# A two-layer decoder trunk in split fp32r: q and k among the conv blocks, rotation halves swapped on ScalarE, high products ahead of low ones

## The chip, the cores and the metric

The kernel runs on one core of a Trainium2 chip. The metric is the device time of one execution in microseconds, the median of several runs. Engines are named as in the profile: PE (TensorE matmuls), PEld (its weight loads), DVE (VectorE), ACT (ScalarE), POOL (GpSimd), SP (SyncE, which issues the DMA loads).

## The reference, cut to what matters

```python
# T = 256 tokens, D = 1024, 2 layers; 4 retention heads, q/k 128 wide, v 256 wide
def hybrid_layer(x, positions, ...):
    proj = rmsnorm(x, norm_mix) @ w_in            # cb cc cu | q k v g | ga gb
    y_conv = (cb * causal_conv3(cc * cu)) @ w_conv_out
    q, k = rotary(q) * 128**-0.5, rotary(k)       # [t1 cos - t2 sin, t1 sin + t2 cos]
    o = retention(q, k, v)                        # decayed q k^T times v, by chunks
    y_ret = (silu(g) * headnorm(o) * ret_norm) @ w_ret_out
    x = x + (sigmoid(ga) * y_conv + sigmoid(gb) * y_ret) @ w_o
    return x + relu(rmsnorm(x, norm_mlp) @ w_up)**2 @ w_down
```

After two layers a last rmsnorm follows. All is float32.

## The kernel before

The activations stand transposed, features on the 128 partitions and the 256 tokens along the free dimension. A weight block is 1 MB: all 1024 inputs of 256 outputs, 16 tiles of 128x128. SP loads it into one of two `raw` buffers; `split_block` cuts each half of it into a high part (ACT rounds to fp32r, line 103) and a low part (DVE subtracts, line 104) in one of three `parts` buffers.

`window` handles one block. With `i` the block's number it first runs the small work that was put down for this point with `at(n, fn)` (n windows later, in order of `ph`), then splits block i+2, then issues the products of block i, then the load of block i+3, then the small products put down with `products_at`. Each engine has its instructions in exactly this order; nothing is rescheduled. In `proj` a block is 32 products: for each of 8 input tiles k and 2 output tiles j one of the high part with high and low activations side by side (512 columns) and one of the low part with the high activations (256 columns), which adds to the second half of the same PSUM tile. The result of a block is taken in the next window by `collect`: ACT copies one half out of PSUM, DVE adds the other.

A layer is 4 blocks for v (`proj_tokens`, 24 products of 512 columns), 28 in the order of `IN_ORDER`, 4 each for `yc` (conv output), `yr` (retention output) and `mg` (merged), 16 for up, 16 for down. In the last layer the last four down blocks go through `proj_one`, with products of 256 columns only. So 72 and 68 blocks, 140 in all, go through `proj`.

Around `q` and `k`, `rotate` (line 448) collects a block, POOL multiplies by the cosine (L451), DVE multiplies the two swapped halves by the sine, 64 partitions at a time (L453, L454), and POOL adds (L455). The tables are multiplied by the norm factor first (`rotations`). The norm factor comes from column sums on PE (`norm_total`), then `factors_begin` and `factors_end` on DVE. In layer 0 POOL computes the angles (`reduce_angles`) meanwhile; the small tiles of this stage share six buffers (tag `tmp1`). For the heads, `head_sums` sums the squares `osq` on PE into `var_ps`, `head_roots` begins an inverse root on DVE and `head_out` multiplies by it, which gives `yr`.

Of the kernel before, what the change touches and what calls it, by code (L numbers as in the profile page):

```python
# [18 lines left out]
P = 128  # L19
# [15 lines left out]
def _conv(i):  # L35
# [5 lines left out]
    + _conv(0) + _conv(1)  # L41
    + [("q", Q0), ("q", Q0 + 256), ("k", K0), ("k", K0 + 256)]
# [10 lines left out]
def trunk_kernel(ctx, tc, px, pos, w, cst, mask, out):  # L53
# [22 lines left out]
    idle = tmp.tile([P, 2 * T], BF16, tag="tmp1", bufs=6, name="idle")  # L76
# [90 lines left out]
    def proj(act, n_blocks=1):  # L167
# [6 lines left out]
        def products(blk, b):  # L174
            for k in range(KT):
                a = act[b].at(k)
                for j in range(2):
                    first, end = b == 0 and k == 0, b == n_blocks - 1 and k == KT - 1
                    mm(ps[:, j], blk[:, 0, 2 * k + j, :], a, first, False)
                    mm(ps[:, j, 1], blk[:, 1, 2 * k + j, :], a[:, 0], False, end)  # L180
# [76 lines left out]
    class Norm:  # L257
# [33 lines left out]
        def split_sum(self):  # L291
            self.sums = tuple(tmp.tile([P, T], F32R, tag="tmp1", bufs=6, name=f"{self.name}_{n}") for n in ("sh", "sl"))
            split(self.sum[:, 0, :], *self.sums)
# [35 lines left out]
    xs = tmp.tile([P, T], F32, tag="tmp1", bufs=6, name="xs")  # L329
# [32 lines left out]
    def late_loads():  # L362
        pos_i = tab["pos"] = tmp.tile([P, T], I32, tag="tmp1", bufs=6, name="pos_i")
# [7 lines left out]
    def reduce_angles():  # L371
        ang, turns, red = (tmp.tile([P, T], F32, tag="tmp1", bufs=6, name=nm) for nm in ("ang", "turns", "red"))
# [13 lines left out]
    def sines():  # L386
        half_sin = tab["sh"] = tmp.tile([P, T], F32, tag="tmp1", bufs=6, name="sh")
# [14 lines left out]
    for layer in range(DEPTH):  # L402
# [6 lines left out]
        def factors_begin(norm=norm):  # L409
            rs_m, rs_a = (tmp.tile([P, T], F32, tag="tmp1", bufs=6, name=n) for n in ("rs_m", "rs_a"))  # L410
# [19 lines left out]
        if layer == 0:  # L430
# [6 lines left out]
            products_at(5, norm_total)  # L437
        else:
            products_at(2, norm_total)
        at(10, rotations)  # L440
# [8 lines left out]
        def rotate(p, ps, cosr, sinr):  # L449
            t, d = collect(ps), qk[:, 2 * p:2 * p + 2, :]  # L450
            nc.gpsimd.tensor_tensor(out=d, in0=t, in1=both(cosr), op=ALU.mult)  # L451
            w_ = t2("rot")
            nc.vector.tensor_tensor(out=w_[0:64], in0=t[64:128], in1=both(sinr[64:128, :]), op=ALU.mult)  # L453
            nc.vector.tensor_tensor(out=w_[64:128], in0=t[0:64], in1=both(sinr[0:64, :]), op=ALU.mult)  # L454
# [122 lines left out]
        def head_roots(i, st):  # L577
# [10 lines left out]
            at(1, lambda: nc.vector.reciprocal(rs, rs))  # L588
            at(2, lambda: newton(rs, t2("rs_a", "rs", 1), rm[:, 1, h, :]))
            for n in range(2):  # L590
                at(2 + n, head_out, 2 * i + n, rs[:, n, :])
# [306 lines left out]
```

## Time and profile before

| what | value |
|---|---|
| median of 3 runs | 906.25 us (905.71 to 907.66) |
| the profiled execution, and its span | 909.5 us, 907.7 us |
| PE busy | 885.3 us, 98% |
| PEld busy | 764.6 us, 84% |
| DVE busy | 709.2 us, 78% |
| ACT busy | 512.9 us, 57% |
| POOL busy | 258.0 us, 28% |
| granted TensorE clock | 0.998 |
| HBM traffic | 179 GB/s over the span |

The span runs from the first instruction to the last; the execution's time has some 2 us around it. A busy share is taken over the whole span, with all its stages. A matmul's end is modelled, so times between products are best read from start to start.

### The profile page before, as it was taken

The page shows a single profiled execution, that of the slowest core. Times are in us where ns is not written, and L with a number is a line of the kernel's source. Part 1 is how long each engine was busy: PE and PEld are TensorE (multiplying, and loading weights), DVE is VectorE, ACT ScalarE, POOL GpSimd, SP SyncE. Part 2 cuts the span into 40 slices and gives each one's busy share as a digit, 9 for nine tenths or more (in the row PEclk, how much of TensorE's full clock was granted, in tenths as well). Part 3 has the DMA queues.
Part 4 walks back from the last instruction along what each step waited for, and adds up shares of the span by engine and source line. Part 5 has one row for each costly group of instructions (what it writes and reads, how often), then busy time and mean ns, then how long its engine had stood idle before and what let it go on. Part 6 is the DMA issues. An engine that isn't in the chain of part 4 may idle for free.

```text
span 907.7 us, 12561 instructions
## 1 busy us (share of the span) xinstructions
PE 885.3 (98%) x5026; PEld 764.6 (84%) x5026; DVE 709.2 (78%) x796; ACT 512.9 (57%) x733; POOL 258.0 (28%) x168
## 2 busy tenths in 40 slices
PE   9988999999999999999999999999999999999996
PEld 6867788878888888888888888888888888888896
DVE  5779999999898766555567999999999896664551
ACT  5835455765556777544445543656665577763350
POOL 0646545422112322100010655452211222220110
PEclk9999999999999999999999999999999999999999
DMA  8534454445654555555555444544465455555531
GB/s 285 189 133 170 168 179 164 183 144 182 232 192 180 195 186 186 197 185 187 187 184 193 156 174 152 190 182 142 159 247 181 185 202 186 186 192 185 183 138 46
DMA packets 23818, 163.00 MB, mean 180 GB/s; under 512 B 2768, under 2 KB 3152, under 8 KB 4432
## 3 DMA queue, kind: packets, MB, share of 16 engines
q1 hardware_dynamic: 23184, 161.36, 50.3%
q10 hardware_dynamic: 576, 0.84, 0.3%
q8 instruction: 39, 0.64, 0.3%
q14 instruction: 19, 0.16, 0.0%
HBM read 161.14 MB, written 1.05 MB: 179 GB/s over the span
## 4 chain that ended last, share of the span: by engine, by line
PE 64%; DVE 23%; issue 4%; POOL 3%; DMA 3%; ACT 2%; SPq 0%; DVEq 0%; ACTq 0%; POOLq 0%
PE ps L165 64%; DVE parts L104 14%; DMA raw<-w 3%; DVE sum L236 2%; DVE rot L454 1%; ACT parts L103 1%; DVE acc L518 1%; DVE yc L104 1%; POOL ta L504 0%; POOL red L369 0%; DVE sg L565 0%; DVE sg L498 0%; DVE acc L521 0%; POOL ang L384 0%; DVE sg L236 0%
## 5 line engine op out<-in xcount | busy, mean ns | idle before, releaser
L104 DVE TENSOR_TENSOR parts<-raw,parts 128x1024 fp32r<-128x1024 f32 x305 | 434.4, 1462 | 90.9 <-ACT parts L103 90.2
L103 ACT CAST parts<-raw 128x1024 fp32r<-128x1024 f32 x305 | 305.9, 1050 | 138.1 <-PE ps L165 85.0
L165 PE MATMUL ps<-mix,parts 128*128 128x512 f32 (+1 forms) x1792 | 322.9, 340 | 11.0 <-DVE parts L104 7.5
L165 PEld LDWEIGHTS ps<-mix,parts 128*128 128x128 f32 x1792 | 274.5, 188 | 54.8 <-DVE parts L104 10.0
L165 PE MATMUL ps<-up,parts 128*128 128x512 f32 (+1 forms) x1088 | 182.3, 330 | 0.0
L165 PE MATMUL ps<-mlp,parts 128*128 128x512 f32 (+1 forms) x1024 | 181.6, 340 | 0.0
L165 PEld LDWEIGHTS ps<-up,parts 128*128 128x128 f32 x1088 | 160.6, 189 | 21.1
L165 PEld LDWEIGHTS ps<-mlp,parts 128*128 128x128 f32 x1024 | 157.0, 188 | 23.8
L236 DVE TENSOR_TENSOR sum<-ps,sum 128x512 f32<-128x512 f32 x78 | 53.3, 684 | 45.5 <-ACT sum L235 45.3
L730 POOL TENSOR_TENSOR u<-u,rr2m 128x512 f32<-128x512 f32 x32 | 46.1, 1441 | 131.3 <-ACT u L729 118.3
L235 ACT COPY sum<-ps 128x512 f32<-128x512 f32 x78 | 45.3, 581 | 51.3 <-PE ps L165 51.3
L285 POOL TENSOR_TENSOR mix_sum<-mix_sum,sq 128x512 f32<-128x512 f32 x8 | 12.6, 1574 | 155.7 <-ACT sq L283 155.6
L165 PE MATMUL ps<-yc,parts 128*128 128x512 f32 (+1 forms) x256 | 45.6, 340 | 0.0
L165 PE MATMUL ps<-yr,parts 128*128 128x512 f32 (+1 forms) x256 | 45.5, 340 | 0.0
L165 PE MATMUL ps<-mg,parts 128*128 128x512 f32 (+1 forms) x256 | 45.5, 340 | 0.0
L165 PEld LDWEIGHTS ps<-yr,parts 128*128 128x128 f32 x256 | 39.2, 188 | 6.0
L165 PEld LDWEIGHTS ps<-yc,parts 128*128 128x128 f32 x256 | 39.2, 188 | 6.0
L165 PEld LDWEIGHTS ps<-mg,parts 128*128 128x128 f32 x256 | 39.2, 188 | 6.0
L165 PE MATMUL ps<-parts,mix 128*128 128x512 f32 x180 | 41.8, 392 | 0.0
L165 PEld LDWEIGHTS ps<-parts,mix 128*128 128x128 f32 x180 | 33.6, 188 | 7.4 <-ACT mix L271 0.2
L694 DVE SCALAR_TENSOR_TENSOR px_sb<-ps,px_sb 128x256 f32<-128x256 f32 x60 | 24.0, 421 | 15.6 <-PE ps L165 14.6
L642 POOL TENSOR_TENSOR sum<-sum,rr 128x512 f32<-128x512 f32 x8 | 15.8, 1979 | 59.2 <-DVE sum L236 59.2
(175 smaller groups left out, 668.1 us busy)
## 6 DMA issues: line engine op xcount, KB each, us to landing
raw<-w SPq DMA_DIRECT2D x151, 1024.0 KB, 4.8
raw<-w SPq DMA_DIRECT2D x2, 256.0 KB, 4.4
raw<-w SPq DMA_DIRECT2D x1, 512.0 KB, 5.6
px_sb<-px SPq DMA_DIRECT2D x1, 512.0 KB, 8.3
mask_sb<-mask SPq DMA_DIRECT2D x1, 512.0 KB, 5.7
out<-o SPq DMA_DIRECT2D x2, 256.0 KB, 2.4
out<-o ACTq DMA_DIRECT2D x2, 256.0 KB, 2.4
px_sb<-px SPq DMA_DIRECT2D x1, 256.0 KB, 5.8
```

Source lines behind the costliest of these rows:

```text
L103: nc.scalar.copy(hi, src)
L104: nc.vector.tensor_tensor(out=lo, in0=src, in1=hi.bitcast(F32), op=ALU.subtract)
L165: nc.tensor.matmul(o, lhsT=a, rhs=b, start=start, stop=stop, skip_group_check=True)
L235: nc.scalar.copy(t, ps[:, :, 1, :])
L236: nc.vector.tensor_tensor(out=t, in0=ps[:, :, 0, :], in1=t, op=ALU.add)
L285: nc.gpsimd.tensor_tensor(out=self.sum, in0=self.sum, in1=sq, op=ALU.add)
L454: nc.vector.tensor_tensor(out=w_[64:128], in0=t[0:64], in1=both(sinr[0:64, :]), op=ALU.mult)
L518: nc.vector.scalar_tensor_tensor(out=acc[:, j, 1:], in0=z[:, j, :T - 1], scalar=w1, in1=acc[:, j, 1:], op0=ALU.mult, op1=ALU.add)
L642: nc.gpsimd.tensor_tensor(out=z, in0=z, in1=both(rr2), op=ALU.mult)
L694: nc.vector.scalar_tensor_tensor(out=xk, in0=ps[:, j, half, :], scalar=scale, in1=xk, op0=ALU.mult, op1=ALU.add)
L730: nc.gpsimd.tensor_tensor(out=u, in0=u, in1=both(rr2), op=ALU.mult)
```

## The change

Six edits. In `proj` the products of a block are issued all high parts first (16 of 512 columns), then all low parts (16 of 256); the first block of `yr`, `mg` and up in each layer (`late`) keeps the order before. q, q, k move from behind the second group of conv blocks to between its blocks. `rotate` now only collects and multiplies by the cosine; one window later `rotate_halves` has ACT copy the two halves across, and POOL multiply by the sine and add; the sign of the table is turned round for this. `head_out` multiplies on POOL, and the reciprocal and what follows it come a window later, the reciprocal between the two halves of a split. The column sums of the norm come after the sixth block of a layer in both layers (in the second it was the third), the tables one window earlier. Scores come one window later. `tmp1` has seven buffers.

```diff
 IN_ORDER = (
     [("g", G0), ("g", G0 + 256)]
-    + _conv(0) + _conv(1)
-    + [("q", Q0), ("q", Q0 + 256), ("k", K0), ("k", K0 + 256)]
+    + _conv(0)
+    + [e for qk, c in zip((("q", Q0), ("q", Q0 + 256), ("k", K0)), _conv(1)) for e in (qk, c)]
+    + [("k", K0 + 256)]
     + _conv(2) + _conv(3)
...
-    def proj(act, n_blocks=1):
+    def proj(act, n_blocks=1, late=False):
...
         def products(blk, b):
-            for k in range(KT):
+            kj = [(k, j) for k in range(KT) for j in range(2)]
+            both_parts = [(k, j, part) for k, j in kj for part in range(2)]
+            for k, j, part in both_parts if late else sorted(both_parts, key=lambda e: e[2]):
                 a = act[b].at(k)
-                for j in range(2):
-                    first, end = b == 0 and k == 0, b == n_blocks - 1 and k == KT - 1
+                first, end = b == 0 and k == 0, b == n_blocks - 1 and k == KT - 1
+                if part == 0:
                     mm(ps[:, j], blk[:, 0, 2 * k + j, :], a, first, False)
+                else:
                     mm(ps[:, j, 1], blk[:, 1, 2 * k + j, :], a[:, 0], False, end)
...
-            products_at(5, norm_total)
-        else:
-            products_at(2, norm_total)
-        at(10, rotations)
+        products_at(5, norm_total)
+        at(9, rotations)
...
             nc.gpsimd.tensor_tensor(out=d, in0=t, in1=both(cosr), op=ALU.mult)
-            w_ = t2("rot")
-            nc.vector.tensor_tensor(out=w_[0:64], in0=t[64:128], in1=both(sinr[64:128, :]), op=ALU.mult)
-            nc.vector.tensor_tensor(out=w_[64:128], in0=t[0:64], in1=both(sinr[0:64, :]), op=ALU.mult)
+            at(1, rotate_halves, p, t, sinr)
+
+        def rotate_halves(p, t, sinr):
+            w_, d = t2("rot"), qk[:, 2 * p:2 * p + 2, :]
+            nc.scalar.copy(w_[0:64], t[64:128])
+            nc.scalar.copy(w_[64:128], t[0:64])
+            nc.gpsimd.tensor_tensor(out=w_, in0=w_, in1=both(sinr), op=ALU.mult)
             nc.gpsimd.tensor_tensor(out=d, in0=d, in1=w_, op=ALU.add)
...
-            at(1, lambda: nc.vector.reciprocal(rs, rs))
-            at(2, lambda: newton(rs, t2("rs_a", "rs", 1), rm[:, 1, h, :]))
+            at(2, lambda: nc.vector.reciprocal(rs, rs), ph=1)
+            at(3, lambda: newton(rs, t2("rs_a", "rs", 1), rm[:, 1, h, :]))
             for n in range(2):
-                at(2 + n, head_out, 2 * i + n, rs[:, n, :])
+                at(3 + n, head_out, 2 * i + n, rs[:, n, :])
...
-            nc.vector.tensor_tensor(out=y, in0=y, in1=both(rs), op=ALU.mult)
+            nc.gpsimd.tensor_tensor(out=y, in0=y, in1=both(rs), op=ALU.mult)
...
-                    products_at(1 + h, scores, h)
+                    products_at(2 + h, scores, h)
...
-            at(0, merge_ret if p < NPAIR - 1 else merge_last, p, proj([yr]))
+            at(0, merge_ret if p < NPAIR - 1 else merge_last, p, proj([yr], late=p == 0))
...
-            at(0, add_to_x, p, proj([mg]), 0.5, norm)
+            at(0, add_to_x, p, proj([mg], late=p == 0), 0.5, norm)
...
-            at(0, up_out, p, proj([norm.act]))
+            at(0, up_out, p, proj([norm.act], late=p == 0))
...
-    cst[:half, 1], cst[half:, 1] = 2.0, -2.0
+    cst[:half, 1], cst[half:, 1] = -2.0, 2.0
```

The first place is PE in a block of `proj`; these are the first products of the g block before, its input tiles 0 to 3 in `mix_103`, the other four in `mix_104`.

```order
L165 MATMUL ps<-mix_103,parts 128x512
L165 MATMUL ps<-mix_103,parts 128x256
L165 MATMUL ps<-mix_103,parts 128x512
L165 MATMUL ps<-mix_103,parts 128x256
L165 MATMUL ps<-mix_103,parts 128x512
L165 MATMUL ps<-mix_103,parts 128x256
```

And this is that whole block and the next one in the change.

```order
L166 MATMUL ps<-mix_103,parts 128x512 x8
L166 MATMUL ps<-mix_104,parts 128x512 x8
L166 MATMUL ps<-mix_103,parts 128x256 x8
L166 MATMUL ps<-mix_104,parts 128x256 x8
L166 MATMUL ps<-mix_103,parts 128x512 x8
L166 MATMUL ps<-mix_104,parts 128x512 x8
L166 MATMUL ps<-mix_103,parts 128x256 x8
L166 MATMUL ps<-mix_104,parts 128x256 x8
```

The two sizes, which took turns, now stand in runs of sixteen. The second place is DVE at the first q blocks of layer 0 (`sum` is a collected block, `rot` the swapped halves, `parts` the low halves of a weight block); before:

```order
L236 TENSOR_TENSOR sum<-ps,sum 128x512
L453 TENSOR_TENSOR rot<-sum,sinq 64x512
L454 TENSOR_TENSOR rot<-sum,sinq 64x512
L104 TENSOR_TENSOR parts<-raw,parts 128x1024 x2
L104 TENSOR_TENSOR q_parts<-qk,q_parts 128x512
L236 TENSOR_TENSOR sum<-ps,sum 128x512
L453 TENSOR_TENSOR rot<-sum,sinq 64x512
L454 TENSOR_TENSOR rot<-sum,sinq 64x512
L104 TENSOR_TENSOR parts<-raw,parts 128x1024 x2
```

In the change, with POOL's rows of the same place behind them:

```order
L242 TENSOR_TENSOR sum<-ps,sum 128x512
L105 TENSOR_TENSOR parts<-raw,parts 128x1024 x2
L242 TENSOR_TENSOR sum<-ps,sum 128x512
L105 TENSOR_TENSOR parts<-raw,parts 128x1024 x2
L105 TENSOR_TENSOR q_parts<-qk,q_parts 128x512
L242 TENSOR_TENSOR sum<-ps,sum 128x512
L105 TENSOR_TENSOR parts<-raw,parts 128x1024 x2
```

```order
L455 TENSOR_TENSOR qk<-sum,cosq 128x512
L462 TENSOR_TENSOR rot<-rot,sinq 128x512
L463 TENSOR_TENSOR qk<-qk,rot 128x512
L650 TENSOR_TENSOR sum<-sum,rr_138 128x512
L455 TENSOR_TENSOR qk<-sum,cosq 128x512
L462 TENSOR_TENSOR rot<-rot,sinq 128x512
L463 TENSOR_TENSOR qk<-qk,rot 128x512
```

The two multiplications have left DVE, POOL has three instructions for a q block where it had two, and a conv block lies between. The third place is DVE around the second sum of squares; before, from the reciprocal of heads 0 and 1 on:

```order
L588 RECIPROCAL rm<-rm 128x512
L565 SCALAR_TENSOR_TENSOR sg<-o_ps,hg,sg 128x256 x2
L236 TENSOR_TENSOR ta<-ps,ta 128x512
L104 TENSOR_TENSOR parts<-raw,parts 128x1024 x2
L241 TENSOR_TENSOR rs_a<-rm 128x512
L242 SCALAR_TENSOR_TENSOR rs_a<-rs_a,rm 128x512
L243 SCALAR_TENSOR_TENSOR rm<-rs_a,rm 128x512
L598 TENSOR_TENSOR sg<-sg,rm 128x512
L104 TENSOR_TENSOR osq<-osq 128x256
```

In the change:

```order
L573 SCALAR_TENSOR_TENSOR sg<-o_ps,hg,sg 128x256 x2
L242 TENSOR_TENSOR ta<-ps,ta 128x512
L105 TENSOR_TENSOR parts<-raw,parts 128x1024 x2
L105 TENSOR_TENSOR osq<-osq 128x256
L242 TENSOR_TENSOR ta<-ps,ta 128x512
L105 TENSOR_TENSOR parts<-raw,parts 128x1024
L596 RECIPROCAL rm<-rm 128x512
L105 TENSOR_TENSOR parts<-raw,parts 128x1024
L247 TENSOR_TENSOR rs_a<-rm 128x512
```

The last split of squares stood behind the reciprocal and the four instructions of its root; now it stands ahead of them.

## Rows read from the trace of the kernel before

**Rows 1.** The page: the span, and each engine's busy time.

```profile
span 907.7 us, 12561 instructions
PE 885.3 (98%) x5026; PEld 764.6 (84%) x5026; DVE 709.2 (78%) x796; ACT 512.9 (57%) x733; POOL 258.0 (28%) x168
```

**Rows 2.** PE in order of time: start, length, instructions, idle before; three stretches.

```profile
209.52 22.78 PE L165 MATMUL ps<-yc,parts 128*128 128x512 f32 x128
232.14 22.77 PE L165 MATMUL ps<-yr,parts 128*128 128x512 f32 x128
...
458.50 16.51 PE L165 MATMUL ps<-parts,mix 128*128 128x512 f32 x72
474.84 0.28 PE L165 MATMUL mix_st<-mix_sh,ones 128*128 128x256 f32 x1
...
880.05 5.92 PE L165 MATMUL ps<-up,parts 128*128 128x256 f32 x48
885.81 0.50 PE L758 MATMUL st<-ones_f,mix_sum 128*128 128x1 f32 x4
```

**Rows 3.** PE in order of time in the first projections of layer 0.

```profile
40.53 11.26 PE L165 MATMUL ps<-mix,parts 128*128 128x512 f32 x64
...
53.60 5.60 PE L165 MATMUL ps<-mix,parts 128*128 128x256 f32 x31 [0.58 <-DVE parts L104]
...
120.54 0.52 PE L165 MATMUL sc_ps<-q_parts,k_parts 128*128 128x256 f32 x3
...
121.04 0.48 PE L165 MATMUL ps<-mix,parts 128*128 128x512 f32 x1
...
127.88 5.80 PE L165 MATMUL ps<-mix,parts 128*128 128x512 f32 x32
```

**Rows 4.** Busy time by stretch: PE, PEld, DVE, ACT, POOL; then clock, DMA share, GB/s.

```profile
60.00:106.00 46.00, 40.50 (x222) 34.01 (x223) 43.23 (x41) 24.23 (x33) 31.16 (x19) 1.00 0.45 161
...
525.00:548.00 23.00, 23.00 (x132) 19.97 (x131) 22.77 (x21) 10.08 (x15) 13.02 (x7) 1.00 0.48 177
720.00:870.00 150.00, 150.00 (x851) 130.20 (x850) 93.63 (x98) 90.23 (x122) 29.12 (x21) 1.00 0.54 188
```

**Rows 5.** DVE and POOL in order of time over one q block of layer 0.

```profile
102.97 0.68 DVE L104 TENSOR_TENSOR q_parts<-qk,q_parts 128x512 fp32r<-128x512 f32 x1
...
104.29 0.69 DVE L453 TENSOR_TENSOR rot<-sum,sinq 64x512 f32<-64x512 f32 x1
104.33 1.80 POOL L451 TENSOR_TENSOR qk<-sum,cosq 128x512 f32<-128x512 f32 x1 [2.36 <-DVE sum L236]
104.99 1.69 DVE L454 TENSOR_TENSOR rot<-sum,sinq 64x512 f32<-64x512 f32 x1
106.71 3.45 DVE L104 TENSOR_TENSOR parts<-raw,parts 128x1024 fp32r<-128x1024 f32 x2
106.83 2.25 POOL L455 TENSOR_TENSOR qk<-qk,rot 128x512 f32<-128x512 f32 x1 [0.69 <-DVE rot L454]
...
110.08 0.68 DVE L104 TENSOR_TENSOR q_parts<-qk,q_parts 128x512 fp32r<-128x512 f32 x1
```

**Rows 6.** DVE in order of time where POOL stands idle.

```profile
662.37 2.36 DVE L104 TENSOR_TENSOR parts<-raw,parts 128x1024 fp32r<-128x1024 f32 x2
```

**Rows 7.** DVE's longest wait between 44 and 60 us: total, times, longest.

```profile
DVE rs_a L241 <- POOL ang L384: 4.2, 1, 4.2
```

**Rows 8.** The heads' factor on DVE: least, median and greatest duration of one (ns).

```profile
L598 DVE TENSOR_TENSOR sg<-sg,rm x8: 678/685/693, 191.2 to 655.3; 128x512 f32<-128x512 f32 x8
```

**Rows 9.** Who waited for whom, whole run: total, times, longest.

```profile
PE ps L165 <- DVE parts L104: 7.5, 8, 1.7
...
PE var_ps L165 <- DVE osq L104: 2.4, 2, 1.6
```

**Rows 10.** The page's groups: busy, mean ns of one, idle before and its cause.

```profile
L235 ACT COPY sum<-ps 128x512 f32<-128x512 f32 x78 | 45.3, 581 | 51.3 <-PE ps L165 51.3
L165 PEld LDWEIGHTS ps<-up,parts 128*128 128x128 f32 x1088 | 160.6, 189 | 21.1
```

More of the change, by code (lines that the diff above doesn't have):

```diff
@@ L75, in trunk_kernel @@
     ones_f = const.tile([P, 1], F32, name="ones_f")
-    idle = tmp.tile([P, 2 * T], BF16, tag="tmp1", bufs=6, name="idle")
+    idle = tmp.tile([P, 2 * T], BF16, tag="tmp1", bufs=7, name="idle")
     cst_sb = const.tile([P, 2], F32, name="cst_sb")
@@ L291, in split_sum @@
         def split_sum(self):
-            self.sums = tuple(tmp.tile([P, T], F32R, tag="tmp1", bufs=6, name=f"{self.name}_{n}") for n in ("sh", "sl"))
+            self.sums = tuple(tmp.tile([P, T], F32R, tag="tmp1", bufs=7, name=f"{self.name}_{n}") for n in ("sh", "sl"))
             split(self.sum[:, 0, :], *self.sums)
@@ L327, in trunk_kernel @@
     nc.scalar.activation(eps2, eps, AF.Square)
-    xs = tmp.tile([P, T], F32, tag="tmp1", bufs=6, name="xs")
+    xs = tmp.tile([P, T], F32, tag="tmp1", bufs=7, name="xs")
     nc.vector.tensor_scalar(out=xs, in0=x[:, 0, :], scalar1=norm.gain[:, 0:1], scalar2=None, op0=ALU.mult)
@@ L362, in late_loads @@
     def late_loads():
-        pos_i = tab["pos"] = tmp.tile([P, T], I32, tag="tmp1", bufs=6, name="pos_i")
+        pos_i = tab["pos"] = tmp.tile([P, T], I32, tag="tmp1", bufs=7, name="pos_i")
         nc.sync.dma_start(out=cst_sb, in_=cst)
@@ L371, in reduce_angles @@
     def reduce_angles():
-        ang, turns, red = (tmp.tile([P, T], F32, tag="tmp1", bufs=6, name=nm) for nm in ("ang", "turns", "red"))
+        ang, turns, red = (tmp.tile([P, T], F32, tag="tmp1", bufs=7, name=nm) for nm in ("ang", "turns", "red"))
         tab.update(ang=ang, turns=turns)
@@ L386, in sines @@
     def sines():
-        half_sin = tab["sh"] = tmp.tile([P, T], F32, tag="tmp1", bufs=6, name="sh")
+        half_sin = tab["sh"] = tmp.tile([P, T], F32, tag="tmp1", bufs=7, name="sh")
         ang, turns = tab["ang"], tab["turns"]
@@ L409, in factors_begin @@
         def factors_begin(norm=norm):
-            rs_m, rs_a = (tmp.tile([P, T], F32, tag="tmp1", bufs=6, name=n) for n in ("rs_m", "rs_a"))
+            rs_m, rs_a = (tmp.tile([P, T], F32, tag="tmp1", bufs=7, name=n) for n in ("rs_m", "rs_a"))
             rsqrt_begin(rr, rs_m, norm.total_ps, 1.0 / D)
@@ L786, in square_last @@
         def square_last(k, ps):
-            sq = tmp.tile([P, T], F32, tag="tmp1", bufs=6, name="sq1")
+            sq = tmp.tile([P, T], F32, tag="tmp1", bufs=7, name="sq1")
             nc.scalar.activation(sq, ps, AF.Square)
```

## The prediction

> **What bounds the kernel now.** I read the busy times first: PE is busy 98% of the span, DVE 78%, ACT 57%, POOL 28% [rows 1]. So a gain must either shorten what PE does or fill the 2% in which it stands. Both are to be found by stage, so I read the stretches next. In the up and down stage (720 to 870 us) PE is busy all the time, while DVE has 94 of 150 us, ACT 90, and the loads half of the DMA time [rows 4]: there the products alone set the pace. PE's own order of time shows that pace: four `yc` blocks, 128 products, take 232.14 - 209.52 = 22.62 us from start to start, which is 5.655 us for a block and 353 ns for a pair of 512 and 256 columns [rows 2].
>
> In the first projections of layer 0 it is otherwise. Between 60 and 106 us DVE is busy 43.2 of 46 us and PE only 40.5 [rows 4]. From 40.53 us (block 6, the first cc) to 127.88 us (block 19) there are 13 blocks and two groups of score products of 121.04 - 120.54 = 0.5 us [rows 3]. At the free pace that is 13 x 5.655 + 1.0 = 74.5 us, and it takes 87.35: PE loses 12.8 us here. Part of it is seen as waits for low parts (7.5 us in 8 waits [rows 9], one of them before 53.60 us [rows 3]), the rest as late starts of blocks, whose PSUM tile is not yet collected. In layer 1, in the same work, PE does not stand although DVE is busy 22.77 of 23 us [rows 4]: there DVE starts the stretch well ahead. Later only the head sums wait, 2.4 us in two waits [rows 9].
>
> **The order of products.** 134 of the 140 blocks through `proj` change (three a layer keep the old order). No row shows a block in the new order, but two show its halves. The v products of layer 1 are 72 products of 512 columns in a row: 474.84 - 458.50 = 16.34 us, 226.9 ns each. In the last two output tiles 48 products of 256 columns stand in a row, each with a weight load of its own: 885.81 - 880.05 = 5.76 us, 120.0 ns each [rows 2]. A new block is then 16 x 226.9 + 16 x 120.0 = 5.55 us against 5.655, and 134 x 0.105 = **14.0 us** less. Below, the bound is nothing, if a product's time depends on what it is and not on its neighbour; I take the rows, since both runs are long and even. What follows PE must keep up: DVE, ACT and the loads have room in the up and down stage [rows 4].
>
> On this the Trainium skill says something else. Its page TensorE: Matmul & The Clock Gate, section Back-to-back issue gap, gives a lone product's gap by its own column count alone; by that the sum of a pair, and so the block, is the same in any order, and this term would be nothing. By the page's formula a pair would take an estimated 325 ns, where the trace has 353, so I hold to the trace.
>
> The new order also moves the need for low parts: the first comes 16 x 0.227 = 3.6 us into the block, the second half's 0.96 us later, at 4.6 us, where it was 16 x 0.177 = 2.8 us. So DVE may be 1.8 us (second half) to 3.6 us (first half) later without stopping PE. It helps once in a stretch where DVE is late throughout. ACT's second high half is needed at 1.8 instead of 2.8 us; ACT is busy 24 of 46 us there [rows 4].
>
> **The buffers.** At 44.9 us DVE waits 4.2 us for POOL to finish the angles, because `rs_a` takes over a `tmp1` buffer that POOL still uses [rows 7]. With seven buffers it takes over that of `pos_i`, which POOL reads only in the first instruction of that chain. All of DVE's work behind it, and with it PE's late blocks, comes 4.2 us earlier. Next late is POOL itself, whose tables are then wanted earlier, but the chain of angles ends before DVE asks for them.
>
> **The rotation.** In a q block before, DVE goes round in 110.08 - 102.97 = 7.11 us: split of the rotated block, add of the collected one, two multiplications (0.69 and 1.69 us), the low halves (3.45 us) [rows 5]. PE's block is 5.655 us, so four rounds cost PE 4 x 1.46 = 5.8 us. The multiplications, 2.38 us, leave. But POOL's work is not free for DVE: the second multiplication, the same as the first, takes 1.00 us more while POOL multiplies beside it, and the pair of low halves 3.45 us beside POOL's add [rows 5] against 2.36 us where POOL is idle [rows 6], 1.09 us more. Two POOL instructions fall on low halves now that did not (the cosine, which lay beside `rot`, and the new product), so DVE takes back 0 to 2.18 us a block. Net relief is 0.2 to 2.38 us a block, 0.8 to 5.8 us for PE in layer 0 (no more than it lost). A conv block now lies between two q or k blocks, and conv blocks with little DVE work fill the round; I take the middle, 3.5 us.
>
> Here the Trainium skill speaks against the change. SBUF — State Buffer, section Who interferes with whom, says that a VectorE instruction with two SBUF inputs contends with a GpSimd instruction that reads SBUF, and that ScalarE waits for no one; by it each new POOL product stops the low splits whenever they meet, the lower end of my 0.2 to 2.38. The trace agrees as to the contention (3.45 against 2.36 us); how often they meet is what no row shows.
>
> ACT gains two copies for a rotation, 16 in all. No row has one of 64 partitions; the copy of 128 takes 0.58 us [rows 10], so 0 to 9.3 us on an engine with 43% idle. A copy stands ahead of the next collect and split in ACT's queue, so these come up to 1.2 us later, and DVE waits for them; that is inside the 3.6 us.
>
> So of the 12.8 us in layer 0: 4.2 from the buffer, 3.5 from the rotation, 1.8 from the later need, **9.5 us**; bounds 4.2 + 0.8 = 5.0 and all 12.8. In layer 1 nothing can be given back, since PE does not stand there.
>
> **The heads.** `head_out` leaves DVE, 8 x 0.685 = 5.5 us [rows 8], and POOL gets eight products of up to 2.25 us, which take back up to 8 x 1.09 = 8.7 us of DVE. PE waits for neither: yr is needed only after the gb and yc blocks. Behind POOL's products stand the gb multiplications, behind them ACT's tanh, its collect and its splits, which PE needs two blocks later. I take nothing; the bound is 2.4 us a layer (the net 1.6 us of DVE, and 0.8 us by which PE is faster over eight blocks). The last split of squares now stands ahead of the root's instructions, and the reciprocal behind it, so the squares come over 2 us earlier (three of some 0.7 us and the factor's 0.685): the **2.4 us** of waits for head sums go, at worst none of it.
>
> **The rest.** Norm sums in layer 1 three blocks later: the factor is first used eight blocks after the layer's start and is ready a block earlier; without that cover a wait of one DVE round. Scores and tables move by a window each, at no price while PE has their inputs. The loads keep their order on SP; 1 MB each 5.55 us instead of 5.655 asks for 2% more than 188 GB/s at half the DMA time [rows 4].
>
> **The sum.** 14.0 + 9.5 + 2.4 = 25.9 us. The profiled execution took 909.5 us, so 883.6 under the profiler; its own time was 3.25 us over the median of 906.25, and against the median the forecast is **880.4 us**.
>
> **The rivals.** (1) The order of products does nothing: a pair costs 353 ns in any order. Then 906.25 - 11.9 = 894.4. (This is the case of the Trainium skill's page on TensorE, above.) For it: no row has the new order; against it: 226.9 + 120.0 = 346.9. (2) POOL takes back what DVE was given: it hits the low halves with each instruction, ACT waits in its queue, and the stretches of gb blocks begin to stand. Then 906.25 - 14.0 - 5.0 - 2.4 + 4.8 = 889.7. For it: the 1.09 us of rows 5 and 6; against it: POOL idles 72% [rows 1]. (3) Slower: low products in a row are shorter than their weight loads. A load takes 189 ns [rows 10]; if each low product took as long, a block is 3.63 + 16 x 0.189 = 6.65 us, one us more, 134 blocks 133 us, and the time 906.25 - 11.9 + 133 = 1027. It decides from 120 + 25.9 / (134 x 16) us, that is 132 ns a product. Against it: 120.0 ns in the last tiles, with a load for each. (4) The change has no effect I can name: 2%.
>
> **How the numbers follow.** Chances: forecast 0.66, rival 1 0.12, rival 2 0.17, rival 3 0.03, no effect 0.02. The forecast alone runs from 906.25 - 14.0 - 2.4 - 12.8 = 877 to 885. The range goes down to 874, since runs of one kernel lie 2 us apart and low products that go to and fro between two PSUM banks may be a little quicker than those of the tail; upwards it takes in rival 2 and most of the way to rival 1: 874 to 893. By the cases: faster by over 0.2% (1.8 us, about what a measurement tells here) 0.95, same 0.02, slower 0.03.
>
> **What the profile after would show.** Right: `yc` and down blocks at 5.55 us from start to start; 13 blocks from the first cc on in some 76 us; no wait of `rs_a` on POOL; no wait of `var_ps`; low halves near 3.45 us still where POOL works. Wrong: blocks at 5.65 (rival 1), waits of PE for low parts or for PSUM in layer 1, or about the first yc blocks (rival 2), low products over 130 ns (rival 3).

## The result, and the profile after

The changed kernel takes 892.8 us (median of four runs, 891.85 to 893.35) where the kernel before took 906.0 in the same session: a ratio of 0.9849 (0.9832 to 0.9866), 13.3 us less. The forecast was 880.4 us in a range of 874 to 893. Sign and range held; half the gain is missing.

First the page: span and busy times, against [rows 1].

```profile
span 890.0 us, 12567 instructions
...
PE 875.0 (98%) x5026; PEld 768.8 (86%) x5026; DVE 705.9 (79%) x772; ACT 523.9 (59%) x749; POOL 294.2 (33%) x184
```

DVE has 24 instructions fewer and only 3.3 us less of work; POOL has 36 us more. PE's busy time fell by 10.3 us, so more than half of the 17.7 us of span is PE's pace, the rest waits.

PE in order of time, against [rows 2, 3]: start, length, instructions, idle before.

```profile
40.71 28.31 PE L166 MATMUL ps<-mix,parts 128*128 128x512 f32 x160
...
73.09 46.37 PE L166 MATMUL ps<-mix,parts 128*128 128x512 f32 x256 [4.07 <-DVE sum L242]
...
199.71 22.43 PE L166 MATMUL ps<-yc,parts 128*128 128x512 f32 x128
221.98 22.55 PE L166 MATMUL ps<-yr,parts 128*128 128x512 f32 x128
244.37 4.63 PE L166 MATMUL ps<-mg,parts 128*128 128x512 f32 x24
250.18 12.09 PE L166 MATMUL ps<-mg,parts 128*128 128x512 f32 x66 [1.18 <-DVE mg L689]
```

Four yc blocks take 221.98 - 199.71 = 22.27 us, 5.567 a block where it was 5.655. From block 6 (first cc) PE needs 79.1 us to block 19, which starts at 119.80, where it was 87.35. One of the two groups of score products that the 87.35 us hold (some 0.5 us each) now falls behind block 19, so for the same work the gain is some 7.7 us and not 8.3. The many short waits for low parts are one long wait for a PSUM tile. Then there is a new wait in the first mg block of layer 0, 1.18 us, with which that block takes 7.33 us instead of 5.65.

All waits of PE after, those of the start and the end of the run left out (total, times, longest): the row on `var_ps` of [rows 9] is gone, and so is that of `rs_a` [rows 7].

```profile
PE ps L166 <- DVE sum L242: 4.1, 1, 4.1
...
PE ps L166 <- DVE mg L689: 1.2, 1, 1.2
```

By place, PE in the profiled executions (909.5 and 891.85 us) is ahead of the kernel before by -0.2 us at block 6, 8.1 at block 19, 9.8 at the first yc block, 9.0 at the first up block, 10.2 at the first down block, 11.9 at layer 1's first g block, 14.9 at its yc blocks, 18.0 at the last tiles. So there are three kinds of gain: 8.3 us in the first projections (7.7 for the same work), some 3.3 us at the head sums of both layers (blocks 28 and 29 fell from 13.63 to 11.58 us, 104 and 105 from 12.82 to 11.58), and a slow drip everywhere else. At the mg blocks 1.7 us are lost.

### The profile page after: what moved, and what is told of

Its sections match the earlier page's. It is cut to its first block, busy times and chain, and to the rows that moved or that the text cites. A ratio compares the mean times of both kernels' runs of the same rounds, so it can differ in the third digit from the quotient of the medians.

```text
span 890.0 us, 12567 instructions
## 1 busy us (share of the span) xinstructions
PE 875.0 (98%) x5026; PEld 768.8 (86%) x5026; DVE 705.9 (79%) x772; ACT 523.9 (59%) x749; POOL 294.2 (33%) x184
## 4 chain that ended last, share of the span: by engine, by line
PE 71%; DVE 17%; POOL 4%; DMA 3%; ACT 2%; issue 2%; SPq 0%; DVEq 0%; ACTq 0%; POOLq 0%
PE ps L166 70%; DVE parts L105 10%; DMA raw<-w 3%; ACT parts L104 1%; DVE sum L242 1%; DVE rm L596 1%; PE o_ps L166 1%; POOL rot L462 1%; POOL qk L455 1%; POOL ta L512 0%; POOL qk L463 0%; DVE acc L526 0%; DVE acc L529 0%; DVE rs_a L247 0%; DVE rs_a L248 0%
## 5 line engine op out<-in xcount | busy, mean ns | idle before, releaser
L166 PE MATMUL ps<-mix,parts 128*128 128x256 f32 (+1 forms) x1792 | 319.0, 339 | 4.9 <-DVE sum L242 4.1
L166 PEld LDWEIGHTS ps<-mix,parts 128*128 128x128 f32 x1792 | 278.6, 190 | 42.9 <-issue 4.2
L166 PE MATMUL ps<-up,parts 128*128 128x256 f32 (+1 forms) x1088 | 179.9, 327 | 0.0
L166 PE MATMUL ps<-mlp,parts 128*128 128x256 f32 (+1 forms) x1024 | 179.0, 337 | 0.0
```

The lines of the kernel that those rows point to most:

```text
L166: nc.tensor.matmul(o, lhsT=a, rhs=b, start=start, stop=stop, skip_group_check=True)
```

## The experiments

In the table, "6 to 19" is the time from the first product of block 6 to that of block 19 of layer 0 in the profile, and the ratio is that to the kernel before in the same session. The first two kernels have two groups of score products in that stretch, the others one.

| kernel | median us (runs) | ratio | 6 to 19 | PE's wait for head sums |
|---|---|---|---|---|
| before_again | 907.98 (902.6 to 910.2) | 1.0002 (0.9977 to 1.0027) | 87.3 | 2.5 |
| group_only | 905.32 (904.0 to 905.8) | 0.9972 (0.9955 to 0.9989) | 85.2 | 6.5 |
| changed kernel | 892.79 (891.9 to 893.4) | 0.9849 (0.9832 to 0.9866) | 79.1 | 0 |
| after_ungrouped | 895.83 (894.2 to 896.6) | 0.9872 (0.9842 to 0.9901) | 80.8 | 0 |
| after_alternating | 890.96 (890.1 to 892.5) | 0.9838 (0.9812 to 0.9864) | 80.7 | 0 |
| after_buf6 | 895.19 (894.5 to 898.8) | 0.9889 (0.9864 to 0.9915) | 82.6 | 0 |
| after_rotate_dve | 897.27 (897.0 to 898.6) | 0.9889 (0.9868 to 0.9910) | 81.8 | 0 |
| after_heads_back | 896.37 (894.6 to 896.7) | 0.9891 (0.9866 to 0.9917) | 79.1 | 4.4 |
| after_heads_mid | 893.61 (893.1 to 894.6) | 0.9850 (0.9826 to 0.9874) | 80.0 | 1.0 |
| after_rot10 | 893.05 (891.9 to 894.1) | 0.9841 (0.9814 to 0.9869) | 78.9 | 0 |
| after_cc_first | 892.73 (891.9 to 893.4) | 0.9854 (0.9829 to 0.9880) | 78.5 | 0 |
| after_tables_pool | 892.80 (891.6 to 893.5) | 0.9836 (0.9815 to 0.9857) | 79.0 | 0 |
| after_gate_mg | 896.52 (895.7 to 896.9) | 0.9879 (0.9851 to 0.9906) | 75.6 | 2.1 |

The changed kernel was timed in the first session only. The differences in us below are of medians from different sessions and chips, between which the median of the kernel before moved from 906.0 to 907.6 us. By the ratios they are 2.1 us and not 3.0 for after_ungrouped, 3.6 and not 2.4 for after_buf6, 3.6 and not 4.5 for after_rotate_dve, 3.8 for after_heads_back and 2.7 and not 3.7 for after_gate_mg. All runs of these five kernels lie above those of the changed kernel, but by the ratios only the interval of after_rotate_dve stands clear of its interval, and those of after_buf6 and after_heads_back just touch it. Where a loss lies is read from one profile of each kernel.

### The order of products: four kernels

**before_again** is the kernel before, unchanged.

> The kernel before, unchanged, for its own scatter. Theory A (the gain of 13.3 us is real in both kernels' medians, and the 909.5 us of the first profiled execution were a chance of that run): about 906 us, and where the profile's blocks of products are slower than 5.655 us or its stalls longer, they tell what a slow execution adds. Theory B (the profiled execution adds some 3 us to each kernel): a profile of 909 us again beside a median of 906.

Its runs lie 8 us apart, and its profile (908.9 us) shows two paces for the same 448 products of the up blocks. PE in order of time, layer 0 and layer 1:

```profile
289.59 79.31 PE L165 MATMUL ps<-mlp,parts 128*128 128x512 f32 x448
368.74 90.61 PE L165 MATMUL ps<-up,parts 128*128 128x512 f32 x512
...
729.27 77.82 PE L165 MATMUL ps<-mlp,parts 128*128 128x512 f32 x448
806.93 72.47 PE L165 MATMUL ps<-up,parts 128*128 128x512 f32 x432
```

From start to start it is 368.74 - 289.59 = 79.15 us for 14 blocks in layer 0, 5.653 a block, and 806.93 - 729.27 = 77.66 us in layer 1, 5.547 a block, nothing between. The granted clock is 1.0 in both. A pair of products costs 353.3 ns at the one pace and 346.7 at the other, and a stretch keeps its pace until a wait or other products come. In the first profile, on which the prediction rests, 103 of the blocks that have no wait and no extra products went at the slow pace and one at the quick pace; here it is 60 and 43. Theory B falls: five of the eleven other runs took longer than the profiled one, so what varies is the kernel, not the profiler. Of theory A the chance is shown, not that slower blocks made the long run, since this profile has fewer of them and is as long: the quick pace brings less than 43 x 0.106 us, as it made PE wait 2.6 us more at layer 1's mg block.

**group_only** is the kernel before with the products in groups and nothing else of the change.

```diff
-            for k in range(KT):
-                for j in range(2):
+            for k, j, part in both_parts if late else sorted(both_parts, key=lambda e: e[2]):
```

> The kernel before with nothing but the order of the products changed. Theory A (grouped blocks take 5.567 us, as in the trace after, against 5.653): 134 x 0.086 = 11.5 us from the pace, and 1 to 3 us more in the first projections, where the low parts are needed later: 891.5 to 893.5 us, which would be all that the whole change gave. Theory B (the order does nothing, the gain came from the other parts): 906 us, blocks of 5.65 us. Theory C (the pace gains 11.5 us but PE, now faster, waits more for DVE elsewhere): 895 to 900 us.

2.2 us less by the medians, though its profile has every grouped block at 5.567 us. Theory C is nearest, and more so than it said. The waits of PE (total, times, longest):

```profile
PE var_ps L165 <- DVE osq L104: 6.5, 2, 4.0
PE ps L165 <- DVE sum L241: 4.6, 2, 2.7
```

PE goes ahead where it may be late with low parts, and stands at the next place where it may not, the head sums: 6.5 us for 2.4 in [rows 9]. The clock takes back more. Behind the second of the waits for `sum` (1.9 us) and behind both of those for the head sums (4.0 and 2.5 us) the granted clock fell to 0.50, the 1.2 GHz level; in the first profile of the kernel before it stayed at full up to the end of the run. Busy time by stretch: PE, PEld, DVE, ACT, POOL; then clock, DMA share, GB/s.

```profile
83.50:86.50 3.00, 3.00 (x9) 2.32 (x8) 3.00 (x3) 1.97 (x2) 1.17 (x2) 0.50 0.00 0
193.20:195.90 2.70, 2.70 (x8) 2.13 (x7) 2.70 (x2) 0.49 (x1) 2.17 (x1) 0.50 0.10 36
629.60:632.80 3.20, 3.20 (x9) 2.42 (x9) 3.20 (x4) 1.57 (x2) 1.58 (x1) 0.50 0.00 0
```

Block 29, behind the first head sum's wait, took 6.93 us and block 105 7.17, where 5.57 is the pace.

**after_ungrouped** was to be the changed kernel in the old order. Its edit (`late=True` as the default) reaches 92 blocks; the 42 yr, mg and up blocks that pass `late` themselves stayed in groups, so the number of blocks in the expectation is wrong.

> The changed kernel with the order of products as before. Theory A (grouping is worth 11.5 us by the pace): 892.8 + 11.5 = 904.3 us, plus up to 3 us of waits for low parts that come back: 904 to 907. The other parts together then gave 0 to 2 us. Theory B (the other parts carry the gain): 893 to 897 us.

It took 3.0 us more by the medians, which the ratios don't tell from nothing. Its projections ran mostly at 5.55 us, its down blocks, which follow grouped blocks, at 5.65.

**after_alternating** has high and low products in turn in all blocks of the changed kernel.

```diff
-    def proj(act, n_blocks=1, late=False):
+    def proj(act, n_blocks=1, late=True):
...
-..., proj([yr], late=p == 0))
+..., proj([yr], late=True))
```

(and the same for mg and up.)

> The changed kernel with high and low products in turn in every block. Theory A (this order has two paces at full clock, 5.547 and 5.653 us a block, and goes from one to the other at a stall, as the profiles of before_again and after_ungrouped show; products in groups have only one, 5.567): runs lie anywhere from 892.8 - 134 x 0.020 = 890 to 892.8 + 134 x 0.086 = 904 us, several us from each other, where runs of the changed kernel lie 1.5 us apart; the profile has whole stretches of blocks at one of the two paces and none between. Theory B (the pace is that of the order alone, 5.653 us): 904 us in every run, with a scatter as small as the changed kernel's.

It is no slower than the changed kernel: 890.96 us, and four of its five runs lie below the lowest of that kernel, though in another session. PE in order of time over the up blocks of layer 0, here and then in the changed kernel:

```profile
280.45 77.81 PE L166 MATMUL ps<-mlp,parts 128*128 128x512 f32 x448
358.11 88.91 PE L166 MATMUL ps<-up,parts 128*128 128x512 f32 x512
```

```profile
279.88 78.09 PE L166 MATMUL ps<-mlp,parts 128*128 128x512 f32 x448
357.81 89.23 PE L166 MATMUL ps<-up,parts 128*128 128x512 f32 x512
```

77.66 us at the quick pace against 77.93 in groups. Here 96 blocks went at the quick pace and 10 at the slow one. The two paces are shown; that its runs would scatter by several us is not so, they lie 2.4 us apart. So in the changed kernel the order of products is worth nothing: groups hold the pace of 5.567 us, and the old order, with most waits gone, falls into its quick pace of 5.547 and loses 1.6 us in the first projections, where it needs low parts early.

### The other parts, undone one at a time

**after_buf6**: six `tmp1` buffers instead of seven.

> The changed kernel with six buffers instead of seven for the tables' intermediates. Theory A (the prediction's: DVE waits 4.2 us again for POOL's angles, all its work in the first projections is later by that): 892.8 + 4.2 = 897. Theory B (half of it, since part of DVE's wait is made up before a block of PE is late): 894.5 to 895.5. Theory C (nothing, another wait stands in its place): 892.8.

The wait is back to the tenth of a us (DVE's waits between 40 and 60 us):

```profile
DVE rs_a L247 <- POOL ang L390: 4.2, 1, 4.2
```

Blocks 6 to 19 take 3.5 us more, and 0.6 us of that return at the mg block of layer 0, which is less late. Of the 3.5 us, 0.6 are block 11, where the granted clock stayed at 0.50 for longer. The median is up by 2.4 us: theory B by the median, between A and B by the profile and the ratio.

**after_rotate_dve**: the rotation's multiplications back on DVE.

```diff
-            at(1, rotate_halves, p, t, sinr)
-...
-            nc.scalar.copy(w_[0:64], t[64:128])
-            nc.scalar.copy(w_[64:128], t[0:64])
-            nc.gpsimd.tensor_tensor(out=w_, in0=w_, in1=both(sinr), op=ALU.mult)
+            nc.vector.tensor_tensor(out=w_[0:64], in0=t[64:128], in1=both(sinr[64:128, :]), op=ALU.mult)
+            nc.vector.tensor_tensor(out=w_[64:128], in0=t[0:64], in1=both(sinr[0:64, :]), op=ALU.mult)
```

> The changed kernel with the rotation of q and k as before: two DVE multiplications instead of two ACT copies and a POOL product, and no window between. Theory A (the prediction's: the rotation off DVE is worth some 3.5 us in layer 0, in bounds of 0.8 to 5.8): 892.8 + 3.5 = 896.3. Theory B (POOL, saturated from 79 to 98 us in the trace after, gives back to DVE as waiting on the low halves what the two multiplications took): 892 to 893.5.

Theory A: 4.5 us more, 2.7 of them between blocks 6 and 19. Some 2.6 us are lost in layer 1, where the kernel before had no wait and the prediction expected no gain: 0.7 us in blocks 92 to 103, and 1.9 us at the mg block, where PE now waits for the last merge as it does in layer 0. PE's waits:

```profile
PE ps L166 <- DVE mg L685: 2.4, 2, 1.2
PE ps L166 <- DVE parts L105: 1.6, 3, 1.0
```

**after_heads_back**: reciprocal, Newton step and scaling of the heads as before.

```diff
-            at(2, lambda: nc.vector.reciprocal(rs, rs), ph=1)
-            at(3, lambda: newton(rs, t2("rs_a", "rs", 1), rm[:, 1, h, :]))
+            at(1, lambda: nc.vector.reciprocal(rs, rs))
+            at(2, lambda: newton(rs, t2("rs_a", "rs", 1), rm[:, 1, h, :]))
...
-            nc.gpsimd.tensor_tensor(out=y, in0=y, in1=both(rs), op=ALU.mult)
+            nc.vector.tensor_tensor(out=y, in0=y, in1=both(rs), op=ALU.mult)
```

> The changed kernel with the head roots and the scaling of the heads as before (reciprocal a block earlier and ahead of the last split of squares, scaling on DVE). Theory A (with the products in groups PE comes to the head sums further ahead of DVE, as in group_only, where these waits took 6.5 instead of 2.4 us): blocks 28 and 104 take 8 to 10 us instead of 6.03, so 4 to 8 us are lost: 897 to 901. Theory B (the heads part is worth what the prediction said, 2.4 us): 895.2. Theory C (its scaling on POOL costs what its order gives, as the late mg block of layer 0 says): within 1 us of 892.8.

3.6 us more, just under A's span; PE's waits for the head sums:

```profile
PE var_ps L166 <- DVE osq L105: 4.4, 2, 3.1
```

The mg block of layer 0 is on time again here (5.65 us), so in the profiles the part gives 6.3 us at the sums of both layers and takes back 1.7. More than 1 us of the 6.3 is the clock: behind the 3.1 us wait it fell to 0.50 here too, and block 29 took 6.72 us.

**after_heads_mid** keeps the reciprocal behind the last split, but a window earlier than the change has it, and scales on DVE.

```diff
-            at(2, lambda: nc.vector.reciprocal(rs, rs), ph=1)
+            at(1, lambda: nc.vector.reciprocal(rs, rs), ph=1)
```

> The changed kernel with the reciprocal still behind the last split of squares, but a window earlier than in the change, and the heads' scaling on DVE. Theory A (the gain of the heads part, 3.6 us by after_heads_back, comes from the order alone, and the late mg block of layer 0, 1.7 us, from the window's delay and POOL): blocks 28 and 104 stay at 6.03 and block 40 at 5.65: 891. Theory B (the delay is what takes the wait away): blocks 28 and 104 at 7 to 10 us, 895 to 897.

Neither: 0.8 us more, which the ratios don't tell from nothing. Its profile is 1.4 us longer, and 0.9 us of that stand at block 11, which the edit doesn't reach (the clock stayed at 0.50 for longer there). The mg block of layer 0 improves from 7.33 to 6.11 us, block 28 goes from 6.03 to 7.34. So of the wait for the head sums (4.4 us) the order takes 3.4 away, and the later window and the scaling on POOL, which were not tried apart, the last 1.0; in layer 0 they lose as much at the merge.

### The wait of 4.1 us in the first projections

I first read it so: the two table products for q stand on DVE, a window earlier than before, between DVE and the sum that collects the PSUM tile of block 8. Three kernels test that.

**after_rot10**

```diff
-        at(9, rotations)
+        at(10, rotations)
```

> The changed kernel with the two table products put back by a window. Theory A (in window 9 they stand between DVE and the sum that collects the PSUM tile of block 8, so that PE waits 4.1 us at block 11 and then has half the clock for 3.4 us, 1.7 us): in window 10 that wait goes or shrinks and the clock stays at full; DVE's 3 us of work remain, so 1.5 to 5 us are gained: 888 to 891. Theory B (DVE is short of time over the whole stretch, and the wait only moves to the next block): 892.8 within 0.8 us, with a wait of about 4 us at block 12.

**after_cc_first**

```diff
-    + [e for qk, c in zip(..., _conv(1)) for e in (qk, c)]
+    + [e for qk, c in zip(..., _conv(1)) for e in (c, qk)]
...
+        at(10, rotations)
```

> The changed kernel with each cc, cu, cb block ahead of its q or k block instead of behind it, and the two table products a window later, so that they are needed a window later too. Theory A (DVE's backlog at blocks 9 to 11 comes from the tables standing in the densest window of layer 0; one window later they meet a block with less work): the waits of blocks 9 to 12 fall from some 6 us to 2 to 3, 888 to 891. Theory B (DVE has the same sum of work up to block 18 and PE waits for it somewhere): 892 to 893.5.

**after_tables_pool**

```diff
-            nc.vector.tensor_tensor(out=cosq, in0=cos_t, in1=rr, op=ALU.mult)
-            nc.vector.tensor_tensor(out=sinq, in0=sin_t, in1=rr, op=ALU.mult)
+            nc.gpsimd.tensor_tensor(out=cosq, in0=cos_t, in1=rr, op=ALU.mult)
+            nc.gpsimd.tensor_tensor(out=sinq, in0=sin_t, in1=rr, op=ALU.mult)
```

(cosk and sink a window later.)

> The changed kernel with the table products of q on POOL too, and those of k a window later. Theory A (the 4.1 us wait at block 11 is the tables' 3.0 us on DVE, ahead of the sum that collects block 8, and the half clock behind it 1.7 us more): DVE gets there 3 us earlier, the wait falls to about 1 us and the clock stays: 888 to 890. Theory B (DVE short of time over the whole stretch, POOL's products slow it as much as its own did): 892 to 893.5, and the wait only moves to block 11 or 12.

All three are within 0.3 us of the changed kernel: theory A fell each time. In after_rot10 the wait became two, of 2.70 and 1.91 us; there and in after_cc_first blocks 6 to 19 gain 0.2 and 0.6 us, and the mg block of layer 0 is 0.7 us later. The third kernel shows what stands behind the tables. POOL, ACT, DVE and PE in order of time around the wait:

```profile
64.44 1.26 POOL L375 TENSOR_SCALAR cos_t<-cos_t 128x256 f32<-128x256 f32 x1
65.67 1.29 POOL L503 TENSOR_TENSOR sg<-sg,rr 128x512 f32<-128x512 f32 x1
...
66.99 0.64 ACT L508 ACTIVATE th<-sg 128x512 f32<-128x512 f32 x1 [4.14 <-POOL sg L503]
...
69.06 0.56 ACT L241 COPY sum<-ps 128x512 f32<-128x512 f32 x1
...
67.66 1.09 DVE L509 SCALAR_TENSOR_TENSOR sg<-th,sg 128x512 f32<-128x512 f32 x1 [2.22 <-ACT th L508]
...
72.35 0.69 DVE L242 TENSOR_TENSOR sum<-ps,sum 128x512 f32<-128x512 f32 x1
...
73.18 40.81 PE L166 MATMUL ps<-mix,parts 128*128 128x512 f32 x224 [3.50 <-DVE sum L242]
```

With the tables gone DVE stands 2.22 us instead, for ACT's tanh; ACT has stood 4.14 us for POOL's gate product, which is queued behind the rotation tables, and the copy with which the collect of block 8 begins (69.06) is queued behind that tanh. Here the wait that PE's row puts down to DVE starts on POOL and passes through two queues. In the changed kernel itself that chain ends a little too early to be seen. ACT and DVE there:

```profile
66.31 0.63 ACT L505 ACTIVATE th<-sg 128x512 f32<-128x512 f32 x1 [4.12 <-POOL sg L500]
...
65.05 1.51 DVE L431 TENSOR_TENSOR cosq<-cos_t,rr 128x256 f32<-128x256 f32 x1 [0.30 <-POOL cos_t L375]
66.48 1.51 DVE L432 TENSOR_TENSOR sinq<-sin_t,rr 128x256 f32<-128x256 f32 x1
67.92 1.23 DVE L506 SCALAR_TENSOR_TENSOR sg<-th,sg 128x512 f32<-128x512 f32 x1
...
70.05 1.37 DVE L529 SCALAR_TENSOR_TENSOR acc<-sum,px_sb,acc 128x254 f32<-128x254 f32 x1
...
72.26 0.69 DVE L242 TENSOR_TENSOR sum<-ps,sum 128x512 f32<-128x512 f32 x1
```

The tanh ends at 66.94 and the second table product at 67.99, and from 65.05 to the collect at 72.26 DVE doesn't stand. So two chains end within about 1 us of each other, DVE's own queue last; with the tables gone the other one shows.

**after_gate_mg** moves the first two gates out of the way, and has a second edit: half of a split goes behind the last merge.

```diff
-                at(0, gate, n, ps, 3 if n < 2 else 0)
+                at(0, gate, n, ps, 14 if n < 2 else 0)
...
+        if i - 1 in hold:
+            split_half(i + 1, 1)
...
-        if i > 2:
+        if i > 2 and i not in hold:
```

(`hold` has the window of each layer's last yr block.)

> The changed kernel with the first two gates' POOL product, tanh and DVE product 11 blocks later, and the second half split of the second mg block behind the last merge instead of ahead of it. Theory A (after after_tables_pool: what holds block 8's PSUM tile is ACT's queue, whose tanh waits 4.1 us for POOL's gate product behind the rotation tables, with the collect's copy behind it): the 4.1 us wait and the half clock go, and from block 6 to block 19 it takes 74 to 76 instead of 79.1 us; the late mg block of layer 0 takes 5.7 to 6.3 instead of 7.33; 886 to 889 us unless DVE, which then has the gates in later blocks, makes blocks 20 to 36 late. Theory B (DVE is short of time over blocks 6 to 36 whatever the order): 79 us may fall, but blocks 28 to 41 take as much longer, 891.5 to 893.5.

Both theories are right in their part, and the kernel is 3.7 us slower. PE in order of time:

```profile
40.68 28.35 PE L168 MATMUL ps<-mix,parts 128*128 128x512 f32 x160
70.49 39.19 PE L168 MATMUL ps<-mix,parts 128*128 128x512 f32 x224 [1.46 <-DVE sum L244]
...
163.38 0.50 PE L168 MATMUL var_ps<-osq,ones 128*128 128x512 f32 x1 [2.11 <-DVE osq L105]
...
272.48 1.66 PE L168 MATMUL ps<-mlp,parts 128*128 128x512 f32 x8 [1.21 <-DVE mlp L284]
274.85 7.28 PE L168 MATMUL ps<-mlp,parts 128*128 128x512 f32 x40 [0.71 <-DVE mlp L284]
```

The wait falls to 1.46 us, the clock stays there, and blocks 6 to 19 take 75.6 us, 3.5 less: moving the gates' work takes most of the wait away. The edit takes POOL's product, the tanh and DVE's product away together, so it doesn't tell which of them does. DVE's rows here, against those of the changed kernel:

```profile
66.47 0.95 DVE L434 TENSOR_TENSOR sinq<-sin_t,rr 128x256 f32<-128x256 f32 x1
...
68.34 0.48 DVE L531 SCALAR_TENSOR_TENSOR acc<-sum,px_sb,acc 128x254 f32<-128x254 f32 x1
...
69.66 0.69 DVE L244 TENSOR_TENSOR sum<-ps,sum 128x512 f32<-128x512 f32 x1
```

The collect comes 2.6 us sooner. DVE's gate product (1.23 us) is gone, the second table product is 0.56 us shorter and a conv product 0.89, which together is as much: DVE's own time and what POOL beside it adds account for the gain. But DVE now has the gates' products where it splits the squares, the head sum is late, and blocks 25 and 26 take 17.8 us instead of 13.9. The other edit gains 0.75 us at the mg block of layer 0, loses 0.3 in layer 1, and makes the first up block late by 2.4 us in both. No version here beats the changed kernel by more than after_alternating's 1.8 us, and the intervals of those two ratios overlap.

## Why the prediction was right in sign and range, and 12.4 us short

In the profiled executions 8.25 us are missing (891.85 for 883.6). Counted for the same work, that is 3.2 in the first projections, 3.5 in the pace elsewhere, 1.7 at the mg blocks, 0.4 at the run's start and end, less some 0.5 that the heads gave over their term. Another 4.2 us lie between those executions and the medians.

**The order of products (14.0 us): the step that failed.** It took 5.655 us as what the old order costs. That was the slow one of two paces, in which the one profiled execution happened to run nearly throughout; so its forecast of the pace after came nearly right by sound sums, and its gain was taken against a pace that the kernel before doesn't always have. The sum of the halves (226.9 + 120.0, a block of 5.55 us) holds, but for the old order's quick pace (5.547); a grouped block takes 5.567, with low products at the tail's 120 ns and high ones at 228.4 instead of 226.9, the dearer ones being the first five of each run (228 to 236 ns), behind the change of size. No run shows low products that are quicker between two PSUM banks, which the range's lower end leaned on. In the profiles the pace gave some 9.2 us outside the first projections, for the same work, where 121 x 0.105 = 12.7 were expected: 2.3 are missing because a block gave 0.086 us and not 0.105, the rest in blocks with score and value products. As a cause the order gave little: 2.2 us alone, where waits and three stretches at half clock took the pace back, and nothing that can be told from it when it is undone in the changed kernel. Rival 1 said just that (894.4 us), for another reason. The Trainium skill's page TensorE: Matmul & The Clock Gate, section Back-to-back issue gap, gives a lone product's gap by its own column count, and by that the order doesn't matter; the quick pace agrees with this (346.7 ns for a pair in turn, 346.9 for its halves in long rows of one size), the slow one doesn't (353.3). Rival 2 named waits in layer 1 or about the first yc blocks, and rival 3 blocks of 6.65 us; the trace shows neither.

**Against the median (3.25 us).** The prediction took the distance of the profiled execution from the median over to the changed kernel, as if the profile added it. It belongs to the scatter of the kernel before (901.9 to 911.9 us over all sessions); the changed kernel's runs lie 1.5 us apart, and its profiled one is the lowest. That makes 3.25 + 0.9 us. That the low runs of before are those with more blocks at the quick pace is an inference: none of them was profiled.

**The first projections (9.5 us).** With the pace, 9.5 + 13 x 0.105 = 10.9 us were expected there, and 7.7 came for the same work. The parts are of the sizes named: buffer 3.5 (forecast 4.2), rotation 2.7 (3.5), later need of low parts 1.6 (1.8), each by undoing it. What the forecast lacked is the wait that then ends last: 4.07 us for DVE, which works through tables, gate and conv products ahead of the collect, with the chain of POOL's gate product and ACT's tanh close behind, and half the clock after it. The prediction named POOL as the next to be late, but asked only whether its tables come in time, not what is queued behind them. "Tables move at no price", which I suspected first, was right by the medians (893.05 us with them moved back).

**The contention.** Low halves beside POOL's new products still take some 3.45 us a pair, as said, and the copies on ACT 0.62 us each, near the 0.58 us of [rows 10]. DVE, ACT and POOL of the changed kernel in order of time, about the first q block:

```profile
78.79 3.46 DVE L105 TENSOR_TENSOR parts<-raw,parts 128x1024 fp32r<-128x1024 f32 x2
...
79.04 0.62 ACT L460 COPY rot<-sum 64x512 f32<-64x512 f32 x1
...
78.94 2.23 POOL L455 TENSOR_TENSOR qk<-sum,cosq 128x512 f32<-128x512 f32 x1 [2.97 <-DVE sum L242]
81.12 2.31 POOL L462 TENSOR_TENSOR rot<-rot,sinq 128x512 f32<-128x512 f32 x1
```

By the Trainium skill's page SBUF — State Buffer, section Who interferes with whom, a VectorE instruction with two SBUF inputs, as the low splits are, contends with a GpSimd instruction that reads SBUF; the trace agrees (3.46 us for the pair here, 2.36 where POOL is idle [rows 6]). The move still pays 4.5 us by the medians, 3.6 by the ratios, since DVE lost two multiplications of 2.38 us for it.

**The heads (2.4 us).** 3.3 us in the profile at the sums, some 3.0 without the pace, against 1.7 lost at the mg blocks, for which the prediction named a bound but took nothing. Undone in the changed kernel the part is worth 3.6.

**Nothing to give back in layer 1.** True of the kernel before, where PE stood at neither place. In the changed kernel the rotation is worth some 2.6 us there too, since PE, sooner, would then wait.

The medians of the parts undone (2.4, 4.5, 3.6, and -1.8 for the order) sum to 8.7 of 13.3 us; by the ratios it is some 10. Parts other than the order were not tried alone on the kernel before, so how much of the rest is the pace that its waits leave behind stays open.

## What to carry to other kernels

A duration that repeats to the nanosecond over a whole profile can still be one of two paces of the same code: before a pace is priced, compare it over several stretches and executions, above all when the kernel's own runs scatter more than its waits explain. Where one engine is near its limit over a long stretch, time that another gains before it returns as a wait at the next place with no slack; so cost a gain up to that place, not at its source. And a wait that a profile puts down to one engine is followed back through the in-order queues behind it (here DVE, ACT, POOL) before an edit is chosen; where two chains end within a us of each other, taking one away gains next to nothing.

## What the hardware showed unexpectedly

Two paces for one sequence of products, at full clock, 5.547 and 5.653 us a block. Of what picks one, the profiles of the old order show only this: behind the token blocks' products of 512 columns the first blocks were always slow; behind two head sums for which PE didn't wait they were quick in all four cases (after_ungrouped and after_alternating, both layers), and behind sums with a wait slow in three of four. The cause stays open, and no kernel forced it.

After the 4.07 us wait of the changed kernel the granted clock fell to 0.50 as in group_only, and block 11 took 7.24 instead of 5.57 us. Busy time by stretch: PE, PEld, DVE, ACT, POOL; then clock, DMA share, GB/s.

```profile
69.00:73.00 4.00, 0.02 (x1) 0.00 (x0) 3.93 (x7) 2.65 (x4) 2.66 (x3) 1.00 0.07 29
74.50:77.00 2.50, 2.50 (x8) 1.91 (x7) 2.50 (x3) 0.99 (x2) 1.48 (x1) 0.50 0.00 0
78.00:80.30 2.30, 2.30 (x19) 2.22 (x18) 2.30 (x4) 2.25 (x4) 1.35 (x1) 1.00 0.93 303
```

So a wait can cost 1.7 us more than its own length. It doesn't follow from the length alone: behind the 2.11 us wait of after_gate_mg the clock fell too (that is part of its 17.8 us) and behind one of 2.66 us in after_cc_first, and behind one of 2.70 us in after_rot10 it did not.
